# Third tile retrieved in the second merge, the table stage written out in turn, and another way of building the gate table

## The chip, the cores and the metric

The kernel runs on one core of one Trainium2 chip. The core has five engines that work side by side, each with its own queue of instructions: TensorE (PE in the profile; PEld is its loading of weights), VectorE (DVE), ScalarE (ACT), GpSimd (POOL) and SyncE (SP, which here only starts transfers). The metric is the device time of one execution in microseconds, as the median of several runs; less is better.

## The reference

The input is 1024 tokens of 1024 channels. A first half of the block (RWKV time mixing beside a sparse attention, merged by gates, then a LayerNorm) gives x; after it comes PEER, an expert layer with 16384 experts, of which each token takes 16 for each of 8 heads. The change bears on how this second part is scheduled and computed:

```python
merged = jax.nn.sigmoid(z_ga) * y_a + jax.nn.sigmoid(z_gb) * y_b
mix = merged @ w_out[l]
x = _layer_norm(DEEPNORM_ALPHA * x + gt1[:, None] * mix, ln1_g[l], ln1_b[l])
...
def _peer(h, w_pq, sub_keys, u_tab, v_tab):
    q = (ht @ w_pq).reshape(T, PEER_HEADS, 2, PEER_HALF)
    s = jnp.einsum('thcd,hcnd->thcn', q, sub_keys)           # 128 keys per half
    s1, i1 = lax.top_k(s[:, :, 0], 16)
    s2, i2 = lax.top_k(s[:, :, 1], 16)
    cand = s1[..., :, None] + s2[..., None, :]
    cand_idx = i1[..., :, None] * 128 + i2[..., None, :]
    top_s, pos = lax.top_k(cand, 16)                         # over 256 pairs
    experts = jnp.take_along_axis(cand_idx, pos, axis=-1)
    gates = softmax(top_s)
    act = gelu(einsum('cd,chkd->chk', hc, u_tab[experts])) * gates
    return einsum('chk,chkd->cd', act, v_tab[experts])
```

An expert's number is (first key i1) x 128 + (second key i2), and a gate is the weight that a token gives to one chosen expert.

## The kernel before

The tokens go in 8 tiles of 128. The first half of the block handles them in two halves of 512; each half ends in `merge(H)`, which multiplies the two branches by w_br_a and w_br_b, gates and adds them, multiplies by w_out, normalizes, and multiplies by the query weights wq (one column block per head h). PE multiplies in three terms (high and low part of weights and activations), here called three-term products.

Retrieval of a tile (`retrieve`, from L1117) is mostly DVE work in 6 steps: scores of the keys by PE, the best 16 of each half by MAX, MATCH_REPLACE and FIND_INDEX, sums of candidate pairs, their best 16, and then the keys i1 and i2 and the gates. The keys are found by `weighted`, which multiplies 0/1 marks by differences and sums each run of 16 by four halving additions (L1192, L1194 to L1196). The retrieval of a tile is a generator; `side` is a chain of such generators that other code advances a step at a time by `next(side)`. With M1 = 3, tiles up to 2 are retrieved inside the merges and tiles 3 to 7 afterwards.

The experts are then computed in two ways. For tiles 0 to 2 (384 tokens) expert rows are gathered: 768 indirect transfers, started by POOL (L1371), each of one row of 1024 numbers per token, each followed by one DVE instruction (L1375 for u, L1379 for v). Rows land in three rooms named g. Rows 0 to 127 run in the first half of the program, rows 128 to 299 in the table stage (below), the others in the dense stage. For tiles 3 to 7 (640 tokens) all experts are computed densely: for each of the 128 first keys i1, `dots_u` multiplies 128 experts' u by all 640 tokens (48 matmuls of 128x320, lines L1285, L1287, L1289), gelu and the gates of that i1 are applied, and `dense_v` multiplies by v (again 48 matmuls for each of 128 units). Weights come in as raw; ACT makes the high part whi and POOL the low part wlo.

The dense way needs a table of gates, indexed by i1, i2 and token. `gate_table` (from L1240) makes it in batches of 8 tokens: 80 batches for the 5 tiles. For each token it makes a row of 0 and 1 that marks i2 (one DVE instruction for all 8, L1247) and a row that holds the gate where the key is i1: six of the 8 tokens by one DVE instruction each (L1252), two by two ACT instructions each (L1254, L1255). A matmul per token (16 PE instructions per batch, L1259) multiplies the two into PSUM, ACT copies two times 128x512 to `st` (L233, st<-tp), and every fourth batch is written to memory (gtD).

The program after the first half has two stages. The table stage holds the retrieval of tiles 3 to 7, the gate table, rows 128 to 299, and the dots of 69 of the 128 first keys ("ahead"; results ds go to memory, dotD). The dense stage holds the other 59 dots, the 128 units of dense_v, and the other rows; it goes over 16 groups of 8 first keys. In each group it loads the gates by `gate_rows` (gt<-gtD).

The order on each engine is made by a scheduler in the build: it simulates times and takes, of what is ready, what stands first in the program. In the table stage the program has retrieval and table first, the 69 dots behind them, the rows last.

## Time and profile before

| what | value |
|---|---|
| runs, us | 3887.53, 4839.4, 3887.27; median 3887.53 |
| profiled execution, us | 3874.22, of which the trace spans 3872.5 |
| busy over the span: PE, DVE | 3549.4 (92%), 2759.5 (71%) |
| busy over the span: ACT, POOL | 1611.5 (42%), 1992.2 (51%) |
| granted clock, mean | 0.955 of full speed |

The trace is of one execution on this one core. A share of busy time is a mean over stages that differ, so the stages are read one by one. In the trace's own time the second merge fills the stretch 1483 to 1683 us, the table stage 1683 to 2469, and the dense stage 2469 to the end. A matmul of four-byte numbers outside the three-term products is two PE instructions in the trace.

### The profile page before, as it was taken

The numbers are of one execution on the slowest core, as the hardware profiler recorded it, in microseconds if no ns is written. First come the engines' busy times: TensorE is split into PE (matmuls) and PEld (weight loads), VectorE is DVE, ScalarE is ACT, GpSimd is POOL, SyncE is SP. The second block draws the span as 40 slices with busy tenths as digits, with TensorE's granted clock in tenths as the row PEclk, the third lists the DMA queues.
The fourth block names the chain that finished last, engine by engine and source line by source line (L and its number), as shares of the span: only waits on it lengthen the run. The fifth ranks groups of instructions, "written<-read, shape, count | busy, mean of one in ns | idle before, by whom it ended". The sixth has DMA issues, their size and how long they took to land.

```text
span 3872.5 us, 65040 instructions
## 1 busy us (share of the span) xinstructions
PE 3549.4 (92%) x24044; PEld 3172.0 (82%) x24045; DVE 2759.5 (71%) x5983; ACT 1611.5 (42%) x2909; POOL 1992.2 (51%) x1566
## 2 busy tenths in 40 slices
PE   8989999888999998779999898899999999999997
PEld 7667776665777776669889898899999999999997
DVE  7856644857377767779999999566676666676654
ACT  3558852343444443426455463622222232222222
POOL 5442222355455543254545454266676676776655
PEclk9999998999999999889999999999999999999998
DMA  7453334765676765477777777688898988998973
GB/s 231 148 151 103 103 98 143 280 188 183 192 222 219 218 220 170 140 258 261 243 259 252 258 273 248 234 301 314 310 332 317 330 313 323 335 323 318 322 266 115
DMA packets 434994, 920.97 MB, mean 238 GB/s; under 512 B 36356, under 2 KB 195412, under 8 KB 431732
## 3 DMA queue, kind: packets, MB, share of 16 engines
q1 hardware_dynamic: 311956, 498.38, 38.5%
q0 software_dynamic: 122720, 418.43, 31.0%
q8 instruction: 190, 3.11, 0.3%
q14 instruction: 128, 1.05, 0.1%
HBM read 791.59 MB, written 125.08 MB: 237 GB/s over the span
## 4 chain that ended last, share of the span: by engine, by line
PE 33%; DVE 21%; DMA 19%; issue 10%; POOL 9%; ACT 4%; SPq 1%; POOLq 0%; ACTq 0%; DVEq 0%
DMA g<-in_v_dram,gidx 4%; PE acc L425 4%; PE acc L426 4%; PE acc L427 4%; DMA g<-in_u_dram,gidx 4%; POOL g L1371 4%; POOL wlo L1272 4%; DVE pg L1379 3%; DMA raw<-in_vt_dram 3%; DMA gt<-gtD 3%; DVE gt L1252 3%; PE pair L1285 2%; PE pair L1287 2%; PE pair L1289 2%; DMA raw<-in_ut_dram 2%
## 5 line engine op out<-in xcount | busy, mean ns | idle before, releaser
L1272 POOL TENSOR_TENSOR wlo<-raw,whi 128x1024 fp32r<-128x1024 f32 x264 | 641.0, 2429 | 285.8 <-ACT whi L233 273.6
L415 POOL TENSOR_TENSOR wlo<-wraw,whi 128x512 fp32r<-128x512 f32 x280 | 372.5, 1333 | 564.0 <-ACT whi L233 496.7
L1371 POOL DMA_INDIRECT g<-in_u_dram,gidx x384 | 403.8, 1052 | 374.0 <-DVE g L1375 211.5
L1371 POOL DMA_INDIRECT g<-in_v_dram,gidx x384 | 388.0, 1011 | 378.3 <-DVE pg L1379 192.2
L1379 DVE SCALAR_TENSOR_TENSOR pg<-g,dots,pg 128x1024 f32<-128x1024 f32 x381 | 489.3, 1284 | 120.3 <-DMA g<-in_v_dram,gidx 113.9
L1285 PE MATMUL pair<-A,whi 128*128 128x320 f32 (+2 forms) x2048 | 483.0, 312 | 38.7 <-DVE A L1317 25.9
L1285 PE MATMUL pair<-h2T,whi 128*128 128x320 f32 x2048 | 479.1, 314 | 17.3 <-DMA h2T<-h2TD 10.0
L1287 PE MATMUL pair<-h2T,whi 128*128 128x320 f32 x2048 | 482.1, 315 | 3.7 <-DMA h2T<-h2TD 3.7
L233 ACT ACTIVATE whi<-raw 128x1024 fp32r<-128x1024 f32 x264 | 278.4, 1056 | 496.2 <-PE pair L1287 194.6
L1287 PE MATMUL pair<-A,whi 128*128 128x320 f32 (+2 forms) x2048 | 480.8, 311 | 0.0
L1289 PE MATMUL pair<-A,wlo 128*128 128x320 f32 (+2 forms) x2048 | 480.2, 311 | 0.5 <-POOL wlo L1272 0.5
L1289 PE MATMUL pair<-h2T,wlo 128*128 128x320 f32 x2048 | 480.4, 314 | 0.0
L1375 DVE SCALAR_TENSOR_TENSOR g<-g,pg 128x1024 f32<-128x1024 f32 x256 | 308.3, 1216 | 106.8 <-DMA g<-in_u_dram,gidx 104.6
L1285 PEld LDWEIGHTS pair<-A,whi 128*128 128x128 f32 x2048 | 348.8, 190 | 43.3 <-issue 29.6
L425 PE MATMUL acc<-big,whi 128*128 128x512 f32 x864 | 356.3, 413 | 23.5 <-DVE zs L533 7.1
L1285 PEld LDWEIGHTS pair<-h2T,whi 128*128 128x128 f32 x2048 | 348.3, 191 | 20.2 <-issue 11.0
L1287 PEld LDWEIGHTS pair<-h2T,whi 128*128 128x128 f32 x2048 | 349.5, 191 | 5.5 <-DMA h2T<-h2TD 4.0
L427 PE MATMUL acc<-big,wlo 128*128 128x512 f32 x864 | 350.7, 406 | 2.4 <-POOL wlo L415 2.4
L426 PE MATMUL acc<-big,whi 128*128 128x512 f32 x864 | 348.9, 404 | 3.6 <-DVE big L451 3.6
L1289 PEld LDWEIGHTS pair<-h2T,wlo 128*128 128x128 f32 x2048 | 348.8, 191 | 1.5
L1289 PEld LDWEIGHTS pair<-A,wlo 128*128 128x128 f32 x2048 | 348.8, 190 | 1.0 <-POOL wlo L1272 1.0
L1287 PEld LDWEIGHTS pair<-A,whi 128*128 128x128 f32 x2048 | 349.2, 190 | 0.0
(482 smaller groups left out, 6650.4 us busy)
## 6 DMA issues: line engine op xcount, KB each, us to landing
raw<-in_vt_dram SPq DMA_DIRECT2D x136, 512.0 KB
raw<-in_ut_dram SPq DMA_DIRECT2D x128, 512.0 KB
gtD<-st SPq DMA_DIRECT2D x20, 2048.0 KB
gt<-gtD SPq DMA_DIRECT2D x32, 1280.0 KB
wraw<-in_wz_dram SPq DMA_DIRECT2D x152, 256.0 KB
dotD<-ds SPq DMA_DIRECT2D x69, 320.0 KB
al<-dotD SPq DMA_DIRECT2D x69, 320.0 KB
mw<-in_wada_dram SPq DMA_DIRECT2D x32, 512.0 KB
```

Source lines behind the costliest of these rows:

```text
L233: copy = lambda o, i, **k: A.activation(o, i, AF.Copy, **k)
L415: G.tensor_tensor(lo, raw, hi.bitcast(F32), op=OP.subtract)
L425: mm(pt, lhsT=wh[:, ks], rhs=ah[:, k, :], start=k == 0, stop=False)
L426: mm(pt, lhsT=wh[:, ks], rhs=al[:, k, :], start=False, stop=False)
L427: ins = mm(pt, lhsT=wl[:, ks], rhs=ah[:, k, :], start=False, stop=k == nk - 1)
L1272: G.tensor_tensor(lo, raw, hi.bitcast(F32), op=OP.subtract)
L1285: mm(pts[n], lhsT=wh, rhs=ah[:, h], start=k == 0, stop=False)
L1287: mm(pts[n], lhsT=wh, rhs=al[:, h], start=False, stop=False)
L1289: mm(pts[n], lhsT=wl, rhs=ah[:, h], start=False, stop=last)
L1371: G.indirect_dma_start(out=u, out_offset=None, in_=a["u" if n < 2 else "v"], in_offset=bass.IndirectOffsetOnAxis(ap=idx[:, k:k + 1], axis=0))
L1375: V.scalar_tensor_tensor(u, u, 1.0, h2, op0=OP.mult, op1=OP.mult, accum_out=dots[:, k:k + 1])
L1379: V.scalar_tensor_tensor(acc, u, dots[:, k:k + 1], acc, op0=OP.mult, op1=OP.add)
```

## The change

- M1 goes from 3 to 4: tile 3 is retrieved in the second merge too. There the retrieval's steps stand after every second block of the merge (4 and 4), and one more after each of the 8 column blocks of wq, where before there were none.
- `weighted` sums each run of 16 by one TENSOR_REDUCE in place of four additions.
- `gate_table`: one DVE instruction per batch marks the first keys of all 8 tokens at once, in bf16, in a layout with the token innermost (hot; keys8 is a constant with each key 8 times). ACT then makes the 8 gate rows, one copy with a scale each, reading every eighth bf16 number. The matmuls write PSUM with a step of four numbers (`tp[:, :, t]`), and the copy to st reads PSUM in a row and writes runs of four numbers.
- The table stage is written out in turn: after each retrieval step three table batches, two dots and five gathered rows, and so on. Rows 128 to 299 get three more rooms, named gx. h2T, the activations that the dots multiply, is loaded by 8 transfers in place of 2.
- The dense stage no longer puts a first key that is not ahead at the head of each group.

```diff
-ONE_HOT = 6
-M1 = 3
+M1 = 4
+GX = 3
...
-            if H or d % QS == QS - 1:
+            if H == 0 or d % 2:
                 next(side, None)
...
-            next(side, None)
+            if H == 0 or d % 2:
+                next(side, None)
...
             nc.sync.dma_start(qTD[H][:, h, :], qt)
+            if H:
+                next(side, None)
...
-            V.tensor_tensor(pr[:, :, 0:8], pr[:, :, 0:8], pr[:, :, 8:16], op=OP.add)
-            s4 = tp_.tile([128, 64, 8], F32, name="wx")
-            V.tensor_tensor(s4[:, :, 0:4], pr[:, :, 0:4], pr[:, :, 4:8], op=OP.add)
-            V.tensor_tensor(s4[:, :, 0:2], s4[:, :, 0:2], s4[:, :, 2:4], op=OP.add)
-            V.tensor_tensor(dst, s4[:, :, 0], s4[:, :, 1], op=OP.add)
+            V.tensor_reduce(dst, pr, axis=AX.X, op=OP.add)
...
+    first_keys = lambda slots: slots[:, 2, 0:64].bitcast(BF)
...
-            oh = du.tile([128, 16, 128], F32, name="gt", bufs=2)
-            V.tensor_tensor(oh[:, 0:8], iota[:, None, :].to_broadcast([128, 8, 128]),
-                            slots[:, 1, b * 8:b * 8 + 8, None].to_broadcast([128, 8, 128]), op=OP.is_equal)
+            room = du.tile([128, 20, 128], F32, name="gt", bufs=2)
+            oh2, oh1 = room[:, 0:8], room[:, 8:16]
+            hot = room[:, 16:20].rearrange("p a b -> p (a b)").bitcast(BF).rearrange("p (a b) -> p a b", b=8)
+            V.tensor_tensor(hot, keys8, k1[:, None, b * 8:b * 8 + 8].to_broadcast([128, 128, 8]), op=OP.is_equal)
+            V.tensor_tensor(oh2, iota[:, None, :].to_broadcast([128, 8, 128]),
+                            slots[:, 0, b * 8:b * 8 + 8, None].to_broadcast([128, 8, 128]), op=OP.is_equal)
             for t in range(8):
-                c = slice(b * 8 + t, b * 8 + t + 1)
-                if t < ONE_HOT:
-                    V.tensor_scalar(oh[:, 8 + t], iotan, slots[:, 0, c], slots[:, 2, c], op0=OP.is_equal, op1=OP.mult)
-                else:
-                    A.activation(oh[:, 8 + t], iota, AF.Square, bias=slots[:, 0, c])
-                    A.activation(oh[:, 8 + t], oh[:, 8 + t], AF.Relu, scale=ng[:, c], bias=slots[:, 2, c])
+                copy(oh1[:, t], hot[:, :, t], scale=slots[:, 1, b * 8 + t:b * 8 + t + 1])
             for u in range(2):
-                tp = ptp()
+                tp = ptp().rearrange("p (a b) -> p a b", b=4)
                 for t in range(4):
-                    mm(tp[:, t * 128:(t + 1) * 128], lhsT=oh[:, 4 * u + t], rhs=oh[:, 8 + 4 * u + t], start=True, stop=True)
+                    mm(tp[:, :, t], lhsT=oh2[:, 4 * u + t], rhs=oh1[:, 4 * u + t], start=True, stop=True)
                 t0 = b % 4 * 8 + 4 * u
-                copy(s_[:, :, t0:t0 + 4].rearrange("p a b -> p b a"), tp.rearrange("p (b a) -> p b a", b=4))
+                copy(s_[:, :, t0:t0 + 4], tp)
...
+            if EARLY <= row < MIDDLE and row % (GB + GX) >= GB:
+                return at["sl"].tile([128, 1024], F32, name="gx", bufs=GX)
...
-        for n in range(2):
-            G.dma_start(h2T[:, n], h2TD[:, n])
+        for k in range(8):
+            G.dma_start(h2T[:, :, k], h2TD[:, :, k])
...
+            def beside(tables, dots, n):
+
                 for g in list(found.values()):
-                    for _ in range(3):
+                    for _ in range(tables):
                         next(g, None)
+                for _ in range(dots):
+                    next(ahead_, None)
+                for _ in range(n):
+                    next(rows)
...
+            for k in range(steps):
+                next(side)
+                beside(3, 2, n)
+            for _ in side:
+                pass
+            for k in range(8):
+                beside(2, 1, n if k < 6 else 0)
...
-                else:
-
-
-                    lead = next(i1 for i1 in first if i1 not in ahead)
-                    first = [lead] + [i1 for i1 in first if i1 != lead]
```

How the order moves shows at three places; these lists count a gate matmul once, so a batch is 8. The first is DVE in the middle of the table stage, before; gt is the room of the one-hot rows, v, s, i and cand belong to the retrieval, and pg is a gathered tile's sum.

```order
L1247 TENSOR_TENSOR gt<-iota,slots 128x1024
L1252 TENSOR_SCALAR gt<-iotan,slots 128x128
L1144 MAX_INDEX i_15924<-v_15923,s_16251 128x8
L1252 TENSOR_SCALAR gt<-iotan,slots 128x128
L1144 MAX_INDEX i_15924<-v_15923,s_16251 128x8
L1153 TENSOR_TENSOR cand<-v_15923 128x8x8
L1144 MAX_INDEX i_15924<-v_15923,s_16251 128x8
L1252 TENSOR_SCALAR gt<-iotan,slots 128x128 x2
L1144 MAX_INDEX i_15924<-v_15923,s_16251 128x8
L1150 TENSOR_TENSOR cand<-v_15923 128x8x16
L1252 TENSOR_SCALAR gt<-iotan,slots 128x128 x2
L1379 SCALAR_TENSOR_TENSOR pg<-g,dots,pg 128x1024
```

The same place on DVE with the change:

```order
L1393 SCALAR_TENSOR_TENSOR pg<-gx,dots,pg 128x1024
L1145 MAX_INDEX i_17628<-v_17627,s_17640 128x8 x3
L1249 TENSOR_TENSOR gt<-keys_15755,slots 128x1024
L1250 TENSOR_TENSOR gt<-iota,slots 128x1024
L1145 MAX_INDEX i_17628<-v_17627,s_17640 128x8
L1393 SCALAR_TENSOR_TENSOR pg<-gx,dots,pg 128x1024
L1393 SCALAR_TENSOR_TENSOR pg<-g,dots,pg 128x1024
L1249 TENSOR_TENSOR gt<-keys_15755,slots 128x1024
L1250 TENSOR_TENSOR gt<-iota,slots 128x1024
L1393 SCALAR_TENSOR_TENSOR pg<-g,dots,pg 128x1024
```

The six L1252 of a batch, strewn between the retrieval's instructions, are gone; a batch is one L1249 and one L1250, and gathered rows from both kinds of rooms stand between the batches.

The second place is PE between the last column of wq (acc) and the first dots (pair), before; L1127 are the retrieval's scores of the keys.

```order
L427 MATMUL acc<-Q,wlo 128x512
L1127 MATMUL tp<-keysT,qT 128x128 x12
L1285 MATMUL pair<-h2T,whi 128x320 x4
L1127 MATMUL tp<-keysT,qT 128x128 x4
L1287 MATMUL pair<-h2T,whi 128x320 x2
L1289 MATMUL pair<-h2T,wlo 128x320 x2
L1285 MATMUL pair<-h2T,whi 128x320 x2
```

The same place on PE with the change (L1233 are the transposes of a retrieved tile's keys and gates, which need its whole retrieval done):

```order
L425 MATMUL acc<-Q,wlo 128x512
L1233 MATMUL tp<-ident,i_15675 128x128
L1233 MATMUL tp<-ident,gates 128x128
L1233 MATMUL tp<-ident,i_15674 128x128
L1128 MATMUL tp<-keysT,qT 128x128 x4
L1284 MATMUL pair<-h2T,whi 128x320 x2
L1286 MATMUL pair<-h2T,whi 128x320 x2
L1288 MATMUL pair<-h2T,wlo 128x320 x2
```

The transposes of tile 3 now stand ahead of the first dots.

The third is PE at the end of the table stage, before; the rows behind the 128 gate matmuls are the first dots of the dense stage.

```order
L1285 MATMUL pair<-h2T,whi 128x320 x2
L1287 MATMUL pair<-h2T,whi 128x320 x2
L1289 MATMUL pair<-h2T,wlo 128x320 x2
L1259 MATMUL tp<-gt 128x128 x128
L1285 MATMUL pair<-h2T,whi 128x320 x2
L1287 MATMUL pair<-h2T,whi 128x320 x2
L1289 MATMUL pair<-h2T,wlo 128x320 x2
```

The end of the table stage on PE with the change:

```order
L1286 MATMUL pair<-h2T,whi 128x320 x2
L1288 MATMUL pair<-h2T,wlo 128x320 x2
L1284 MATMUL pair<-h2T,whi 128x320 x2
L1286 MATMUL pair<-h2T,whi 128x320 x2
L1288 MATMUL pair<-h2T,wlo 128x320 x2
L1258 MATMUL tp<-gt 128x128 x8
L1284 MATMUL pair<-h2T,whi 128x320 x2
L1286 MATMUL pair<-h2T,whi 128x320 x2
```

Before, the last 128 gate matmuls stand in one block behind all 69 dots of this stage; now they stand in pieces between the last dots.

## Rows read from the trace of the kernel before

**Rows 1.** Stages: length, busy time (instructions) by engine, clock, DMA share, GB/s.

```profile
1483.00:1683.00 200.00, 151.90 (x645) 116.61 (x643) 146.40 (x660) 79.06 (x136) 61.74 (x47) 0.85 0.49 160
1683.00:2469.00 786.00, 695.48 (x4731) 675.05 (x4731) 763.69 (x1920) 412.21 (x691) 367.44 (x239) 0.95 0.73 251
2469.00:3872.50 1403.50, 1337.90 (x9017) 1330.90 (x9016) 909.88 (x1130) 388.14 (x478) 921.66 (x672) 0.98 0.84 302
```

**Rows 2.** A wait of PE, table stage: waiter, what released it, us, times, longest.

```profile
PE tp L1236 <- DVE i L1196: 32.5, 8, 7.7
```

**Rows 3.** DVE groups, table stage: busy us, mean ns, idle before.

```profile
L1252 DVE TENSOR_SCALAR gt<-iotan,slots 128x128 f32<-128x128 f32 x480 | 190.6, 472 | 0.0
...
L1379 DVE SCALAR_TENSOR_TENSOR pg<-g,dots,pg 128x1024 f32<-128x1024 f32 x127 | 162.7, 1281 | 6.8 <-DMA g<-in_v_dram,gidx 6.1 <-DVE wp L1190 0.2
...
L1247 DVE TENSOR_TENSOR gt<-iota,slots 128x1024 f32<-128x1024 f32 x80 | 104.9, 1311 | 2.8 <-ACT gt L1255 2.8
...
L1194 DVE TENSOR_TENSOR wx<-wp 128x256 f32<-128x256 bf16 x30 | 30.1, 1002 | 0.7
L1192 DVE TENSOR_TENSOR wp<-wp 128x512 bf16<-128x512 bf16 x30 | 25.2, 839 | 0.4
L1195 DVE TENSOR_TENSOR wx<-wx 128x128 f32<-128x128 f32 x30 | 23.7, 790 | 0.7
...
L1184 DVE TENSOR_TENSOR ge<-wx,ranks 128x1024 bf16<-128x1024 bf16 x20 | 13.8, 692 | 0.5
...
L1196 DVE TENSOR_TENSOR i<-wx 128x64 f32<-128x64 f32 x20 | 13.7, 683 | 0.2
...
L1214 DVE TENSOR_REDUCE gs<-gates 128x8 f32<-128x128 f32 x5 | 1.4, 285 | 0.7 <-ACT gates L1212 0.7
```

**Rows 4.** PE and ACT groups, table stage.

```profile
L1259 PE MATMUL tp<-gt 128*128 128x128 f32 x1280 | 177.2, 292 | 52.8 <-DVE gt L1252 40.0 <-ACT st L233 12.8
...
L233 ACT ACTIVATE st<-tp 128x512 f32<-128x512 f32 x159 | 164.7, 1110 | 118.9 <-PE tp L1259 118.4
...
L233 ACT ACTIVATE whi<-raw 128x1024 fp32r<-128x1024 f32 x70 | 73.8, 1054 | 98.9 <-PE pair L1287 65.9 <-issue 25.0 <-DMA raw<-in_ut_dram 5.7
L1255 ACT ACTIVATE gt<-gt,slots,ng 128x128 f32<-128x128 f32 x160 | 70.4, 489 | 8.0 <-DVE ng L1243 7.7 <-ACT ds L233 0.3
...
L1254 ACT ACTIVATE gt<-iota,slots 128x128 f32<-128x128 f32 x160 | 52.6, 386 | 0.0
...
L233 ACT ACTIVATE ds<-pair 128x640 f32<-128x640 f32 x69 | 47.4, 687 | 0.0
...
L233 ACT ACTIVATE slots<-tp 128x128 f32<-128x128 f32 x5 | 1.4, 273 | 17.9 <-PE tp L1236 17.9
```

**Rows 5.** PE timeline, gate batch among dots: start us, us, instructions.

```profile
1995.85 1.95 PE L1259 MATMUL tp<-gt 128*128 128x128 f32 x16
1997.55 0.39 PE L1285 MATMUL pair<-h2T,whi 128*128 128x320 f32 x1
1997.78 0.46 PE L1287 MATMUL pair<-h2T,whi 128*128 128x320 f32 x2
...
1999.83 0.46 PE L1289 MATMUL pair<-h2T,wlo 128*128 128x320 f32 x2
```

**Rows 6.** PE timeline, the last gate batches of the table stage.

```profile
2418.58 3.78 PE L1259 MATMUL tp<-gt 128*128 128x128 f32 x16 [4.67 <-DVE gt L1252]
...
2467.01 2.05 PE L1259 MATMUL tp<-gt 128*128 128x128 f32 x16 [0.97 <-ACT st L233]
```

**Rows 7.** A stretch inside the second merge, columns as in group 1.

```profile
1490.00:1580.00 90.00, 74.01 (x309) 55.84 (x308) 89.11 (x465) 31.34 (x55) 27.73 (x20) 0.91 0.43 134
```

**Rows 8.** PE timeline at the start of the table stage.

```profile
1679.81 1.40 PE L1285 MATMUL pair<-h2T,whi 128*128 128x320 f32 x4 [10.02 <-DMA h2T<-h2TD]
```

**Rows 9.** Waits of PE, dense stage.

```profile
PE pair L1285 <- DVE A L1317: 29.5, 16, 6.6
```

**Rows 10.** Waits of DVE, dense stage.

```profile
DVE pair L1315 <- DMA gt<-gtD: 85.1, 16, 18.2
```

More of the change, by code (lines that the diff above doesn't have):

```diff
@@ L1369, in peer_gather @@
                     idx = index(row)
-                u = grow() if row < MIDDLE or row % (GB + GM) < GB else dv.tile([128, 1024], F32, name="g2", bufs=GM)
+                u = room(row)
                 G.indirect_dma_start(out=u, out_offset=None, in_=a["u" if n < 2 else "v"],
@@ L1407, in out_rows, with finish @@
         nc.sync.dma_start(out[r0:r0 + n, :], dst[p])
-    def finish(i, acc, dv, rows):
+    def finish(i, acc, at):
         last = i == NG - 1
-        row, xa = ((dv.tile([128, 2 * DN], F32, name="A", bufs=AB)[:, 0:1024] if last else grow()) for _ in range(2))
+        row, xa = ((at["dv"].tile([128, 2 * DN], F32, name="A", bufs=AB)[:, 0:1024] if last else grow()) for _ in range(2))
         mod_row(row, 2)
@@ L1417, in finish @@
         V.tensor_tensor(y2, y2, xa, op=OP.add)
-        g, b = rows[0:2] if last else (grow(), grow())
+        g, b = at["ln"][0:2] if last else (grow(), grow())
         if not last:
@@ L1608, in body @@
             st = sl.tile([128, 2, 128, 32], F32, name="st")
+            keys8 = sl.tile([128, 128, 8], BF, name="keys8")
+            copy(keys8, iota[:, :, None].to_broadcast([128, 128, 8]))
             found = {}
@@ L1618, in body, with dots_ahead @@
             side = retrieve_all(range(M1, 8), tk, table)
-            live = True
-            while live:
-                live = next(side, side) is not side
+            more = {"du": du, "sl": sl, "pg": pg}
+            rows = gather_all(more)
+            for _ in range(EARLY):
+                next(rows)
+            def dots_ahead():
+                for i1 in ahead:
+                    ds = sl.tile([128, DN], F32, name="ds", bufs=4)
+                    copy(by_half(ds), dots_u(i1, du, h2T, 2))
+                    nc.sync.dma_start(dotD[ahead[i1]], ds)
+                    yield
+            ahead_ = dots_ahead()
+            def beside(tables, dots, n):
                 for g in list(found.values()):
-                    for _ in range(3):
+                    for _ in range(tables):
                         next(g, None)
+                for _ in range(dots):
+                    next(ahead_, None)
+                for _ in range(n):
+                    next(rows)
+            steps = 6 * (8 - M1)
+            n = (MIDDLE - EARLY) // (steps + 6)
+            for k in range(steps):
[5 more added lines that the diff above has]
+                beside(2, 1, n if k < 6 else 0)
+            for _ in range(MIDDLE - EARLY - n * (steps + 6)):
+                next(rows)
             for g in found.values():
@@ L1627, in body @@
                     pass
-            mark("dots")
-            for i1 in ahead:
-                ds = sl.tile([128, DN], F32, name="ds", bufs=4)
-                copy(by_half(ds), dots_u(i1, du, h2T, 2))
-                nc.sync.dma_start(dotD[ahead[i1]], ds)
+            for _ in ahead_:
+                pass
         tkp.__exit__(None, None, None)
@@ L1671, in body @@
             mark("gather")
-            for i in range(NG):
-                finish(i, peer_gather(i, du, dv, pg), dv, ln)
+            more.update(dv=dv, ln=ln)
+            for _ in rows:
+                pass
     mark("end")
```

37 lines of the change are left out of this document (22 added, 15 removed).

## The prediction

> **What bounds the kernel now.** I read the table by stages first [rows 1]: what is to be seen there is which engine has no time left. In the dense stage it is PE: 1337.9 of 1403.5 us busy, at 0.98 of full clock. In the table stage it is DVE: 763.7 of 786 us (97%), while PE is busy for 695.5 and ACT for 412.2. So the table stage is the place where less DVE work can show in the time, and in the dense stage it can't.
>
> The second view is what PE waits for in the table stage [rows 2, 4]: 40.0 us for one-hot rows by L1252, and 32.5 us for the last addition of the retrieval's sums (L1196); both are DVE. The third is what the same PE work needs when nothing holds it. In the timeline [rows 5] seven pairs of dots' matmuls start between 1997.78 and 1999.83: 2.05 / 14 = 0.146 us each, so 48 x 0.146 = 7.03 us for a unit of dots, and a gate batch between them takes 1997.55 - 1995.85 = 1.70 us. The stage has 69 dots and 80 batches: 485 + 136 = 621 us. That is 79% of its 786. The dense stage has 59 + 128 = 187 units, 1315 us, which is 94% of its 1403.5 [rows 1]. The gap between 79% and 94% is what there is to win. The last place to look at is the end of the table stage [rows 6]: from 2418.58 to 2469 PE has gate batches alone, 16 of them for 27 us of work, at first held by DVE and then by ACT's copies to st (a batch each 3.05 us: 2.05 of work and 0.97 of waiting).
>
> **The change part by part: DVE in the table stage.** Taken out: 190.6 us of L1252; 25.2 + 30.1 + 23.7 + 13.7 = 92.7 us of halving additions [rows 3]; and tile 3's share of the rest of the retrieval, which is what 763.7 leaves without these, the one-hot rows of L1247 (104.9) and the gathered rows of L1379 (162.7): 212 us for five tiles. Added: 80 marks of first keys (128x1024 in bf16) and 24 reduces for four tiles. A mark is nearest to L1184, the comparison of 128x1024 bf16, 0.69 us; its f32 cousin L1247 takes 1.31, so 55 to 105 us, and I take 55. No reduce of 128x1024 is shown; the small one, L1214 with 128x128, takes 0.285 us, and eight of these would be 2.28; the cheapest pass over 1024 numbers is 0.69. So 17 to 55 us, and I take 31 (1.3 each, as L1247, which also goes through f32). With a fifth of 212 us gone, DVE comes to 764 - 191 - 93 + 55 + 31 - 42 = about 525 us (at the upper prices 600). That is below PE's 621 in either case, so DVE stops being the bound, and PE or ACT comes next.
>
> **ACT in the table stage.** Taken out: 52.6 + 70.4 us of L1254 and L1255 and 164.7 us of copies to st, which leaves 124.5. Added: 640 copies of one gate row, and 160 copies to st in the new order [rows 4]. A copy with a scale of 128x128 that reads PSUM in a row takes 0.273 us (slots<-tp); the two activations on 128x128 take 0.386 and 0.489. The copy to st now takes 1.11 us for 512 numbers written with a step of 128 bytes, while ds takes 0.687 us for 640 numbers in a row, so 0.55 for 512: the step costs (1.11 - 0.55) / 512 = 1.1 ns a number. I take the same for the new read, which steps by 16 bytes: 0.273 + 0.14 = 0.41 us, in a range from 0.27 to 0.53, and 0.55 for the new copy to st in a range from 0.55 to 1.11. A batch then takes ACT 8 x 0.41 + 2 x 0.55 = 4.4 us (3.3 to 6.5), all 80 of them 350 us, and ACT comes to 475 of some 690. [...]
>
> What counts is the stretches with gates. In the changed order of PE 20 of the 69 dots have no gate matmul near them, so the 80 batches lie beside 49 dots. PE needs 49 x 7.03 + 136 = 480 us there; ACT 80 x 4.4 + 49 x (1.05 + 0.69) for whi and ds = 437. PE is late by a little, so the new ACT work is hidden, but narrowly; at 6.5 us a batch it would be 605 and not hidden.
>
> **PE in the table stage.** Its work stays as it is, if a matmul that writes PSUM with a step of four costs what it did. No matmul of before does that, so the bounds are 0 and a doubling. The block of 16 batches at the end gets dots between its pieces, which takes its 28 us of waiting. With DVE at 525 and ACT at 475, I take a share of 90% for PE's 621: between now and the dense stage, nearer to the latter, as score matmuls, transposes and some waits for the retrieval stay. 621 / 0.90 = 690 us, **96 us less**. By the dense stage's 94% it is 661, by 86% it is 722.
>
> **The gathered rows** are as many as before. POOL has 367.4 of 786 us of work and DVE now has room; the six rooms let loads run ahead, which is worth nothing as neither is the bound. The same bytes in 690 us are a DMA share of 0.73 x 786 / 690 = 0.83, which the dense stage has already (0.84) [rows 1]. Zero, then, between -5 and +10.
>
> **Second merge and the start of the dots.** From 1490 to 1580 DVE is busy for 89.1 of 90 us and PE for 74.0 [rows 7], so retrieval steps hold the merge there. Half of them move behind wq's columns; PE can gain its 16 us, and up to some 25 with the stretches around. Then the first dots wait for h2T, 10.0 us in one piece at 1679.81 [rows 8], loaded as two large pieces; eight pieces by k let the first products start at the first one. Against it: tile 3's transposes stand ahead of the first dots, so PE waits for its whole retrieval, a third one in a stretch that had two. A tile's retrieval is (212 + 93) / 5 = 61 us of DVE before, and the stretch of wq in which DVE had little to do is shorter than that. So I give the first dots 13 us and not 25, in a range from -28 to +7.
>
> **Dense stage.** Without the reordering, each group begins with ahead keys. PE loses 29.5 us in 16 waits for A [rows 9], most of them behind DVE's wait for the gates' load (85.1 us in 16, [rows 10]), because before a group's first key and the ahead ones came from two different loads. That load now has the time of a few units more. But the unit of dots at the group's head, 7 us, which covered gelu and gates of the others, is gone. I take -10, in a range from -30 to +15.
>
> **Sum.** -96 - 13 - 10 = -119, and two microseconds back for rounding of stages that overlap: -117. The profiled execution of 3874.2 becomes 3757, and the median of the runs, which is 13.3 us above it, 3887.5 - 117 = **3770** us. With the ends of the terms together, taken as partly independent, this forecast goes from 3715 to 3825.
>
> **Rivals.** First, the written step makes the gate matmuls dearer (slower than before). For it: the operation is new, and 1280 instructions stand on the bounding engine. Against it: in the timeline a gate instruction of 128 columns takes 0.106 us beside dots that take 0.146 for 320 columns [rows 5], so these matmuls aren't limited by the pace of their columns' writes alone. With k times the price the stage is (485 + 136k) / 0.90: at k = 2 that is 841, +55, less 23 for the other two parts: about +32, **3920**. From k = 1.8 on it eats the whole gain. [...]
>
> Second, ACT becomes the bound where the gates are. At the upper price the 49 dots with gates take 605 in place of 480 us: the stage is 690 + 125 = 815, and with the other parts the time is 3887.5 + 29 - 23 = 3894; at 5.4 us a batch (8 x 0.53 + 2 x 0.55) it is 517, +37, which is 3807. I give this case, at its middle, **3850**. For it: the price of a read by steps isn't shown, and ACT works in order, so whi for the next dots queues behind eight gate rows. Against it: the 40.0 us of waiting for DVE falls away whatever ACT does.
>
> Third, the change does less than it says: tile 3 holds PE at the start for the 30 us that DVE needs, and the first dots come at 1700 in place of 1670: **3800**.
>
> **How the numbers follow.** A measurement of this kernel can tell about 2% from no change, which is 78 us: faster is below 3810, slower above 3965. The forecast has 0.66, the second rival 0.13, the third 0.09, the first 0.12. Faster: nine tenths of the forecast, a third of the second rival and most of the third: 0.71. Slower by over 2% needs k above 2.3 in the first rival: 0.04. Same is the rest, 0.25. The range is 3715 to 3850: it takes in the forecast's own range, the third rival and the milder half of the second.
>
> **What would show it.** Right: the table stage is 690 us long, DVE is busy for near 525 of it, PE's share is 0.90, no wait for one-hot rows by DVE is left, and no block of gate batches stands alone at the end. A gate row by ACT takes 0.41 us and a copy to st 0.55. Wrong: a gate batch that takes 3 us and more on PE without any wait (first rival); PE's waits on gt released by ACT, above 50 us in sum (second); a PE wait of 20 us and more for tile 3's keys, ahead of the first dots (third). A dense stage that grows by over 15 us would show that the head of each group was worth more than the gate load's wait.

## The result, and the profile after

The changed kernel takes 3747.99 us in the median of four runs (3743.65 to 3754.99), the kernel before 3889.49. The ratio is 0.964, 95% interval 0.9619 to 0.966: faster by 3.6%, 141.5 us where 117 were forecast. The ratio leaves out the one execution of the kernel before that took 4839.4 us. The profiled execution went from 3874.22 to 3743.65 us, its span from 3872.5 to 3741.9, which is 130.6 us; two later comparisons, each beside the kernel before, gave 128 and 127 us (a_changed and e6 in the table below).

The table of stages of the kernel after has the columns of [rows 1]: length, busy time and instructions of PE, PEld, DVE, ACT and POOL, granted clock, DMA share, GB/s. The upper bounds are the same event, the end of what stands ahead of the dense stage. The lower ones are not quite: 1677 is the start of the first dots, while 1683 of before lies 3.2 us behind it (1679.81, [rows 8]), and 1483 is a round number in both.

```profile
1483.00:1677.00 194.00, 144.13 (x625) 109.30 (x623) 172.54 (x751) 84.54 (x143) 69.19 (x55) 0.85 0.57 185
1677.00:2367.00 690.00, 664.00 (x4734) 650.02 (x4735) 569.68 (x1294) 490.03 (x1002) 349.14 (x235) 0.99 0.78 281
2367.00:3741.90 1374.90, 1333.36 (x9008) 1329.82 (x9006) 915.10 (x1130) 387.68 (x477) 924.51 (x673) 0.99 0.86 307
```

Beside [rows 1] the table stage is shorter by 96 us (786 to 690; from the first dots on it is 789 to 690), the dense stage by 28.6 (1403.5 to 1374.9). The 6 us of the second merge (200 to 194) are not what the merge gained, as is shown below. DVE is busy for 569.7 of 690 us, 83% and no longer 97%. PE's idle time in the table stage went from 786 - 695.5 = 90.5 to 690 - 664 = 26 us; the other 31.5 us are less busy time for nearly as many instructions (4731 and 4734), at a granted clock of 0.99 in place of 0.95. The clock can be most of that, by an estimate from these rows: 695.5 x 0.95 / 0.99 = 667. But a gate batch that stands alone also counts as busy for longer (2.05 us) than one between dots (1.70) [rows 5, 6], so the share of the clock isn't shown. In the dense stage 24 of the 28.6 us are idle time of PE.

The costliest groups of the table stage after, as in [rows 3, 4] (busy us, mean ns, idle before):

```profile
L232 ACT ACTIVATE gt<-gt,slots 128x128 f32<-128x128 bf16 x640 | 274.4, 517 | 62.3 <-DVE gt L1249 55.9 <-issue 2.5 <-DVE i L1145 1.9
...
L1258 PE MATMUL tp<-gt 128*128 128x128 f32 x1280 | 161.7, 279 | 14.2 <-ACT st L232 11.5 <-ACT sc L232 2.5
...
L232 ACT ACTIVATE st<-tp 128x512 f32<-128x512 f32 x160 | 87.4, 586 | 24.0 <-PE tp L1258 22.0 <-issue 1.5 <-PE pair L1286 0.4
L1393 DVE SCALAR_TENSOR_TENSOR pg<-gx,dots,pg 128x1024 f32<-128x1024 f32 x64 | 81.9, 1280 | 3.0 <-DMA gx<-in_v_dram,gidx 2.4
...
L1249 DVE TENSOR_TENSOR gt<-keys,slots 128x1024 bf16<-128x1024 bf16 x80 | 67.8, 852 | 50.5 <-issue 21.9 <-ACT gt L232 18.8 <-PE tp L1258 7.5
...
L1193 DVE TENSOR_REDUCE i<-wp 128x64 f32<-128x1024 bf16 x16 | 19.4, 1214 | 0.3
```

A gate row by ACT takes 0.517 us from its start to its end, but the rows of a batch overlap: 274.4 us for 640 are 0.43 each. A copy to st takes 0.586 us in place of 1.110 (87.4 / 160 = 0.55 with the overlap), a mark 0.85, a reduce 1.21. PE's 40.0 us of waiting for one-hot rows is gone; 14.2 us are left, nearly all for ACT. DVE hardly waits for rows of experts (3.0 us in the row of gx). It now waits for ACT, 31.4 us for the retrieval's scores (sc) and 18.8 for gate rows in L1249's row:

```profile
DVE v L1137 <- ACT sc L232: 31.4, 12, 5.6
```

At the start of the stage PE's timeline and its waits, from 1460 to 1677, show the third rival's wait:

```profile
1643.52 0.40 PE L425 MATMUL acc<-Q,wlo 128*128 128x512 f32 x1
...
1674.93 0.45 PE L1233 MATMUL tp<-ident,i 128*128 128x128 f32 x1 [31.01 <-DVE i L1193]
```

```profile
PE tp L1233 <- DVE i L1193: 31.0, 1, 31.0
```

wq's products end at 1643.9 (1664.9 before), and then PE stands for 31.0 us until tile 3's keys are there. The wait for h2T [rows 8] is hidden behind it. Of the 21 us between these two ends 6.3 lie ahead of the merge, whose first product starts at 1483.9 before and at 1477.6 here. They can't be put down to the change: in a_changed, the changed kernel run again, it starts at 1485.8. Counted from its first product, the merge up to the end of wq, and then the time to the first dots, are, before:

```profile
1483.90:1664.90 181.00, 146.12 (x607) 112.11 (x605) 132.04 (x563) 73.83 (x125) 53.04 (x40) 0.87 0.44 141
1664.90:1679.80 14.90, 2.32 (x24) 1.80 (x25) 13.80 (x94) 4.68 (x9) 7.76 (x6) 0.68 0.92 341
```

and after:

```profile
1477.60:1643.90 166.30, 147.44 (x637) 111.88 (x635) 147.60 (x702) 75.92 (x133) 52.52 (x40) 0.92 0.50 157
1643.90:1676.90 33.00, 1.99 (x13) 1.44 (x12) 27.79 (x55) 10.52 (x13) 19.26 (x17) 0.55 0.94 331
```

The merge gains 14.7 us and the wait takes 18.1, so the first dots come 3.4 us later in the merge's own time (6 in a_changed).

In the dense stage PE's wait for A (the dense activations, made of dots and gates), 29.5 us in 16 before [rows 9], is now

```profile
PE pair L1284 <- DVE A L1316: 18.3, 8, 4.3
```

and DVE's waits there have no row for gt's load any more [rows 10]. PE's wait for A is 11 of the 24 us of idle time; what the rest was stays open.

### The profile page after: what moved, and what is told of

Read it like the earlier page. It is cut to its first block, busy times and chain, and to the rows that moved or that the text cites. A ratio compares the mean times of both kernels' runs of the same rounds, so it can differ in the third digit from the quotient of the medians.

```text
span 3741.9 us, 64784 instructions
## 1 busy us (share of the span) xinstructions
PE 3505.2 (94%) x24045; PEld 3139.0 (84%) x24045; DVE 2596.4 (69%) x5433; ACT 1695.7 (45%) x3230; POOL 1981.3 (53%) x1572
## 3 DMA queue, kind: packets, MB, share of 16 engines
q0 software_dynamic: 124608, 418.43, 31.4%
## 4 chain that ended last, share of the span: by engine, by line
PE 49%; DVE 14%; DMA 13%; issue 8%; POOL 7%; ACT 6%; SPq 0%; POOLq 0%; ACTq 0%; DVEq 0%
PE pair L1284 7%; PE pair L1286 7%; PE pair L1288 7%; PE acc L423 4%; PE acc L424 4%; PE acc L425 4%; POOL g L1385 3%; DMA g<-in_u_dram,gidx 3%; DMA raw<-in_vt_dram 3%; POOL wlo L1271 3%; DMA g<-in_v_dram,gidx 3%; PE tp L1258 2%; DMA raw<-in_ut_dram 2%; ACT gt L232 2%; PE acc L975 2%
## 5 line engine op out<-in xcount | busy, mean ns | idle before, releaser
L1385 POOL DMA_INDIRECT g<-in_u_dram,gidx x361 | 373.6, 1035 | 298.4 <-DVE g L1389 180.5
L1393 DVE SCALAR_TENSOR_TENSOR pg<-g,dots,pg 128x1024 f32<-128x1024 f32 x317 | 407.1, 1284 | 123.1 <-DMA g<-in_v_dram,gidx 118.0
L1284 PE MATMUL pair<-h2T,whi 128*128 128x320 f32 x2048 | 475.6, 312 | 0.2 <-ACT ds L232 0.2
L1286 PE MATMUL pair<-h2T,whi 128*128 128x320 f32 x2048 | 473.3, 311 | 0.0
L1385 POOL DMA_INDIRECT g<-in_v_dram,gidx x320 | 307.7, 961 | 170.8 <-DVE pg L1393 80.8
L1389 DVE SCALAR_TENSOR_TENSOR g<-g,pg 128x1024 f32<-128x1024 f32 x233 | 281.0, 1216 | 118.4 <-DMA g<-in_u_dram,gidx 116.8
L1284 PEld LDWEIGHTS pair<-h2T,whi 128*128 128x128 f32 x2048 | 344.6, 189 | 1.6 <-ACT ds L232 0.4
L1286 PEld LDWEIGHTS pair<-h2T,whi 128*128 128x128 f32 x2048 | 343.9, 189 | 1.0
```

Source lines behind the costliest of these rows:

```text
L1284: mm(pts[n], lhsT=wh, rhs=ah[:, h], start=k == 0, stop=False)
L1286: mm(pts[n], lhsT=wh, rhs=al[:, h], start=False, stop=False)
L1385: G.indirect_dma_start(out=u, out_offset=None, in_=a["u" if n < 2 else "v"], in_offset=bass.IndirectOffsetOnAxis(ap=idx[:, k:k + 1], axis=0))
L1389: V.scalar_tensor_tensor(u, u, 1.0, h2, op0=OP.mult, op1=OP.mult, accum_out=dots[:, k:k + 1])
L1393: V.scalar_tensor_tensor(acc, u, dots[:, k:k + 1], acc, op0=OP.mult, op1=OP.add)
```

## Experiments

For each kernel the table gives medians and ratios, and of its profiled execution "first dots" (start of the first product on h2T) and "first A" (start of the first copy of a dense activation); between them lies the table stage. The first row is the kernel before, in the trace of [rows 1]; a_changed is the changed kernel once more. The first dots of one and the same kernel differ by 11 us from execution to execution (changed and a_changed), mostly by what lies ahead of the second merge, so the lengths of stages say more than the starts.

| kernel | median us | ratio to before, 95% | first dots | first A | table stage | first A to end |
|---|---|---|---|---|---|---|
| before | | | 1679.8 | 2484.9 | 805.1 | 1387.6 |
| changed | 3747.99 | 0.9640, 0.9619 to 0.9660 | 1676.9 | 2377.9 | 701.0 | 1364.0 |
| a_changed | 3749.20 | 0.9663, 0.9626 to 0.9699 | 1688.1 | 2389.9 | 701.8 | 1356.8 |
| e1_late_transposes | 3736.41 | 0.9643, 0.9615 to 0.9671 | 1649.1 | 2353.7 | 704.6 | 1357.4 |
| e10_late_again | 3738.77 | 0.9642, 0.9603 to 0.9682 | 1659.5 | 2366.6 | 707.1 | 1359.1 |
| e2_old_gate_table | 3788.53 | 0.9774, 0.9745 to 0.9802 | 1689.4 | 2421.7 | 732.3 | 1373.2 |
| e3_lead_back | 3774.62 | 0.9737, 0.9707 to 0.9766 | 1687.3 | 2384.1 | 696.8 | 1392.6 |
| e4_tile3_back | 3776.12 | 0.9728, 0.9692 to 0.9763 | 1659.0 | 2404.1 | 745.1 | 1367.3 |
| e5_new_gates_alone | 3891.62 | 1.0051, 1.0028 to 1.0073 | 1681.2 | 2499.4 | 818.2 | 1390.2 |
| e12_retrieval_alone | 3815.28 | 0.9837, 0.9816 to 0.9858 | 1678.8 | 2417.6 | 738.8 | 1383.9 |
| e9_old_turn | 3776.72 | 0.9735, 0.9694 to 0.9775 | 1679.7 | 2414.2 | 734.5 | 1358.3 |
| e8_three_rooms | 3783.12 | 0.9746, 0.9726 to 0.9766 | 1686.1 | 2423.4 | 737.3 | 1364.7 |
| e7_old_sums | 3789.32 | 0.9772, 0.9750 to 0.9794 | 1701.6 | 2419.3 | 717.7 | 1364.4 |
| e6_contiguous | 3750.28 | 0.9662, 0.9632 to 0.9693 | 1684.6 | 2385.8 | 701.2 | 1365.6 |

Three groups ran side by side with the kernel before: e1, e2, e3, e5 (before 3875.17 us), a_changed, e4, e9, e10 (3877.39), and e6, e7, e8, e12 (3877.50). e6 is the changed kernel but for a layout that cost nothing (0.9662 beside a_changed's 0.9663), and stands for it in its group.

**The gate table: e2 and e5.** e2 is the changed kernel with the old table:

```diff
-            V.tensor_tensor(hot, keys8, k1[:, None, b * 8:b * 8 + 8].to_broadcast([128, 128, 8]), op=OP.is_equal)
...
-                copy(oh1[:, t], hot[:, :, t], scale=slots[:, 1, b * 8 + t:b * 8 + t + 1])
+                if t < ONE_HOT:
+                    V.tensor_scalar(oh[:, 8 + t], iotan, slots[:, 0, c], slots[:, 2, c], op0=OP.is_equal, op1=OP.mult)
+                else:
+                    A.activation(oh[:, 8 + t], iota, AF.Square, bias=slots[:, 0, c])
+                    A.activation(oh[:, 8 + t], oh[:, 8 + t], AF.Relu, scale=ng[:, c], bias=slots[:, 2, c])
...
-                    mm(tp[:, :, t], lhsT=oh2[:, 4 * u + t], rhs=oh1[:, 4 * u + t], start=True, stop=True)
+                    mm(tp[:, t * 128:(t + 1) * 128], lhsT=oh[:, 4 * u + t], rhs=oh[:, 8 + 4 * u + t], start=True, stop=True)
```

> The changed kernel, all but the gate table, which is the one of before (six of eight gate rows by DVE, two by ACT in two instructions, PSUM written in a row). Theory (the table stage was bound by DVE's work): DVE's 570 us in the stage lose 68 and get 191, so 693, which is the whole of the present 690; the stage grows to about 725 to 735 and the time to 3780 to 3795. Rival (the order written out in turn gave the gain): the stage stays within 10 us of 690 and the time within 10 of the changed kernel's 3748.

3788.53 us, as the first theory had it: the stage is longer by 31 us (701 to 732), a little less than the 35 to 45 expected. The windows of e2's table stage, and PE's waits there:

```profile
1689.40:2421.70 732.30, 687.54 (x4802) 672.82 (x4801) 693.52 (x1699) 410.30 (x684) 361.45 (x236) 0.97 0.77 267
```

```profile
PE tp L1258 <- DVE gt L1251: 31.7, 15, 3.5
```

DVE is busy for 693.5 of 732.3 us (693 expected) and PE waits for its gate rows again. Against a_changed's ratio the old table costs 0.0111 x 3876 = 43 us in this order. e5 is the other half, the kernel before with nothing but the new table:

```diff
-                if t < ONE_HOT:
-                    V.tensor_scalar(oh[:, 8 + t], iotan, slots[:, 0, c], slots[:, 2, c], op0=OP.is_equal, op1=OP.mult)
...
+            V.tensor_tensor(hot, keys8, k1[:, None, b * 8:b * 8 + 8].to_broadcast([128, 128, 8]), op=OP.is_equal)
...
+                copy(oh1[:, t], hot[:, :, t], scale=slots[:, 1, b * 8 + t:b * 8 + t + 1])
```

> The kernel before with the new gate table alone (marks of first keys in one DVE instruction, gate rows by ACT, PSUM written by steps); order, M1, sums, rooms and dense stage as before. Theory: DVE's work in the table stage falls from 764 to about 640, and the dots with gates beside them run at PE's pace; but 16 batches still stand alone at the end, and there ACT needs 8 x 0.517 + 2 x 0.586 = 5.3 us a batch, 85 us in place of 55. The stage comes to 715 to 740, the time to 3820 to 3845. Rival (the order gave the gain): stage above 765, time above 3868. If the block at the end doesn't matter: stage near 690 and time near 3790.

It is slower than before (1.0051). Here my theory fell: DVE has 631.7 us of work in place of 765, and the stage is 818 us in place of 805. What PE and DVE wait for, in e5's table stage:

```profile
PE tp L1261 <- ACT st L233: 38.9, 22, 5.3
PE tp L1236 <- DVE i L1196: 35.1, 5, 11.4
```

```profile
DVE pg L1381 <- DMA g<-in_v_dram,gidx: 49.9, 26, 5.4
...
DVE g L1377 <- DMA g<-in_u_dram,gidx: 17.0, 9, 5.8
```

PE waits for ACT where it waited for DVE, and as long (38.9 us for 40.0). DVE, with time of its own, now stands for 66.9 us on rows of experts that haven't landed, where before it was 11.2 us:

```profile
DVE pg L1379 <- DMA g<-in_v_dram,gidx: 6.1, 5, 2.0
DVE g L1375 <- DMA g<-in_u_dram,gidx: 5.1, 4, 2.2
```

And the block at the end is worse than it was in [rows 6]; PE's timeline:

```profile
2467.17 2.05 PE L1261 MATMUL tp<-gt 128*128 128x128 f32 x16 [0.47 <-ACT st L233]
2471.49 2.05 PE L1261 MATMUL tp<-gt 128*128 128x128 f32 x16 [2.26 <-ACT st L233]
2475.76 2.80 PE L1261 MATMUL tp<-gt 128*128 128x128 f32 x16 [2.22 <-ACT st L233]
2480.02 3.78 PE L1261 MATMUL tp<-gt 128*128 128x128 f32 x16 [1.46 <-ACT st L233]
```

A batch there takes 4.27 us, which is ACT's eight gate rows and two copies (5.3 were expected, from the times of single ones, which overlap), where one of before took 3.05: for the 16 batches that is some 20 us. Less work on the busiest engine gave nothing. I read this as three other things standing close behind it: ACT's rows in the block, rows that land late, and the end of the retrieval. e5 alone doesn't show it; the runs below undo them one by one.

**The retrieval: e12, e4, e7.** e12 is the kernel before with the retrieval's edits alone:

```diff
-M1 = 3
+M1 = 4
...
+            if H:
+                next(side, None)
...
-            V.tensor_tensor(pr[:, :, 0:8], pr[:, :, 0:8], pr[:, :, 8:16], op=OP.add)
...
+            V.tensor_reduce(dst, pr, axis=AX.X, op=OP.add)
```

> The kernel before with the retrieval's edits alone: M1 = 4, the merge's steps in their new places, sums by one reduce; the gate table, the order of the table stage, three rooms, h2T's two loads and the dense stage as before. The block of 16 gate batches behind the last dots is gone from its order of PE. Theory B (the stage of before was as long as the retrieval took, plus that block; either gets shorter only by less retrieval work in the stage): from first dots to first A 735 to 765 us in place of 805, less what PE waits for tile 3 at the start (25 to 35 us, in place of 14 for h2T), ratio 0.980 to 0.992. Theory D (DVE's work is what counts, and the gate rows were most of it): DVE still has 191 us of gate rows, some 660 in all, and the stage stays above 780, ratio above 0.993.

0.9837 and a stage of 738.8 us: theory B, with the old gate rows still on DVE. The block is gone (the last gate batch starts at 2346.7, with dots behind it up to the stage's end), and of the 127 us of e6, beside it, these edits alone give 62. PE's waits in e12's table stage and ahead of it:

```profile
PE tp L1235 <- DVE i L1195: 36.3, 9, 22.7
PE tp L1258 <- DVE gt L1251: 31.0, 23, 3.1
```

PE still waits for DVE's gate rows (31.0 us), as in e2. e4 puts only tile 3 back into the table stage of the changed kernel:

```diff
-M1 = 4
+M1 = 3
```

> The changed kernel with M1 = 3: tile 3 is retrieved in the table stage again, all else as changed, the stage written out in turn too. In its order of PE the last 128 gate matmuls stand in one block again. Theory B (tile 3's earlier retrieval is what shortened the stage): the block costs what it costs in the kernel before with the new gate table, 16 x 4.3 = 68 us for 27 of work; DVE has one more retrieval to do; the table stage comes to 745 to 790, ratio 0.975 to 0.988. Theory A (the order written out in turn did it): stage within 15 us of 701, ratio within 0.004 of the changed kernel's.

The stage is 745 us (theory B), and the block is there again, in PE's timeline:

```profile
2377.97 2.89 PE L1258 MATMUL tp<-gt 128*128 128x128 f32 x16 [2.23 <-ACT st L232]
2382.23 3.74 PE L1258 MATMUL tp<-gt 128*128 128x128 f32 x16 [1.37 <-ACT st L232]
2386.49 2.05 PE L1258 MATMUL tp<-gt 128*128 128x128 f32 x16 [0.52 <-ACT st L232]
```

But the first dots come 29 us earlier, since no transposes stand ahead of them. So the ratio rose by 0.0065, 27 us, less than theory B's low end: tile 3's earlier retrieval gives 43 us in the stage and pays 29 for it at the start. That leaves 14 us at the first A; from there to the end e4 takes another 10.5 more than a_changed, for which no cause is shown. e4 also has the merge's new places and h2T's eight transfers without tile 3: its first dots come 177.1 us after the merge's first product, 195.9 before and 199.3 in the changed kernel. What each of these two edits gives wasn't tested by itself. e7 is the changed kernel with the old sums:

```diff
-            V.tensor_reduce(dst, pr, axis=AX.X, op=OP.add)
+            V.tensor_tensor(pr[:, :, 0:8], pr[:, :, 0:8], pr[:, :, 8:16], op=OP.add)
...
+            V.tensor_tensor(dst, s4[:, :, 0], s4[:, :, 1], op=OP.add)
...
```

> The changed kernel with the four halving additions in place of one reduce. DVE gets about 3 us more for each of 24 sums in the table stage (four additions of 3.1 us in all for one reduce of 1.2, some 45 us in the stage) and some 6 sums' worth, 11 us, on the path of tile 3 ahead of the first dots. Theory: with DVE at 570 of 701 us only the start shows: 8 to 14 us, ratio higher by 0.002 to 0.004. Rival (the retrieval's own length still sets the stage): 25 us and more, ratio higher by 0.007.

39 us more than e6, beside it: the time is the rival's. The sums lengthen the retrieval itself, and PE waits for its end at each tile:

```profile
PE tp L1237 <- DVE i L1197: 63.4, 5, 42.8
```

63.4 us in 5, the first 42.8, against 42.3 in 5 with 33.6 in e6. The first dots are 17 us later than in e6, of which 5 lie ahead of the merge, and the stage is 16.5 longer, though DVE is busy for only 581 of its 718 us.

**Rooms and turn: e8 and e9.** e9 has the table stage in the old writing, and three rooms; e8 has the new writing and three rooms:

```diff
-GX = 3
+GX = 0
...
```

and e9 besides, with the rows written behind the dense stage:

```diff
...
+            live = True
+            while live:
+                live = next(side, side) is not side
                 for g in list(found.values()):
-                    for _ in range(tables):
+                    for _ in range(3):
                         next(g, None)
...
-            for k in range(steps):
-                next(side)
-                beside(3, 2, n)
...
+            for i1 in ahead:
+                ds = sl.tile([128, DN], F32, name="ds", bufs=4)
+                copy(by_half(ds), dots_u(i1, du, h2T, 2))
+                nc.sync.dma_start(dotD[ahead[i1]], ds)
...
+            for _ in gather_all({"du": du, "pg": pg, "dv": dv, "ln": ln}):
```

> The changed kernel, with the table stage written as before (retrieval and tables first, then the 69 dots, all gathered rows at the end of the program, three rooms in place of six); M1 = 4, sums, gate table, h2T's loads and the dense stage are the changed ones. In its order of PE no block of gate batches stands at the end. Theory A (writing the stage out in turn is what shortened it): the table stage, 701 us from first dots to first A, grows to 750 or more, ratio above 0.977. Theory B (tile 3's earlier retrieval did it, since the retrievals then end while dots are left to put between the last batches): stage below 725, ratio below 0.971.

> The changed kernel with three rooms for rows in the table stage in place of six, the order written out in turn. The kernel with the old order and three rooms was 27 us behind the changed one. Theory A (the turn is what counts): the same time as the changed kernel, within 5 us. Rival (the rooms are what counts, since a DVE instruction on a row that hasn't landed holds up the retrieval and the marks behind it): 15 to 25 us more, and DVE's waits for rows above 40 us in the table stage.

e9's stage of 734.5 us lies between its two theories. e8 settles it: 737.3 us, as slow as e9, so with three rooms writing the stage out in turn gives nothing, and the rooms are worth 36 us of stage (33 us of time against e6). DVE's waits in the middle of e8's stage:

```profile
DVE pg L1393 <- DMA g<-in_v_dram,gidx: 54.5, 30, 7.5
...
DVE g L1389 <- DMA g<-in_u_dram,gidx: 20.2, 10, 5.7
```

74.7 us in 40 waits on rows that haven't landed, in which DVE stands idle with the retrieval and the marks queued behind the row. With six rooms the changed kernel has 3.9 us of it; from 1700 to 2370, the window of e8's rows, a_changed has 2.8 and e6 1.6. With three rooms e5 has 66.9 us in its stage, and e12 23.6 from 1700 to 2370 with DVE busy for 672 of its stage's 739 us; the kernel before, with DVE busy for 765 of 805 us, has 11.2. Whether six rooms would do the same with the rows written last wasn't tried.

**The dense stage: e3.**

```diff
+                else:
+                    lead = next(i1 for i1 in first if i1 not in ahead)
+                    first = [lead] + [i1 for i1 in first if i1 != lead]
```

> The changed kernel with the dense stage's old order inside a group: the first key that is not ahead stands first again. The dense stage got 28.6 us shorter with the change (1403.5 to 1374.9). Theory: the order inside the groups did it (29.5 us of PE waits for A in 16 became 18.3 in 8, and clock dips behind these waits went): dense stage 1390 to 1403, time 3765 to 3775. Rival: a steadier table stage and fewer transfers at the stage's start did it: dense stage stays within 8 us of 1375, time within 8 of 3748.

From first A to the end it takes 1392.6 us, 28.6 more than the changed kernel, and the wait for gates is back:

```profile
DVE pair L1314 <- DMA gt<-gtD: 62.9, 15, 7.1
```

```profile
PE pair L1284 <- DVE A L1316: 37.9, 13, 4.3
```

That is as the theory had it, and by the ratios the old order costs (0.9737 - 0.9663) x 3876 = 29 us. The table above agrees without exception: the four kernels with the old order in a group need 1383.9 to 1392.6 us there, the others 1356.8 to 1373.2.

**PSUM written by steps: e6.**

```diff
-                tp = ptp().rearrange("p (a b) -> p a b", b=4)
+                tp = ptp().rearrange("p (b a) -> p b a", b=4)
...
-                    mm(tp[:, :, t], lhsT=oh2[:, 4 * u + t], rhs=oh1[:, 4 * u + t], start=True, stop=True)
+                    mm(tp[:, t, :], lhsT=oh2[:, 4 * u + t], rhs=oh1[:, 4 * u + t], start=True, stop=True)
...
-                copy(s_[:, :, t0:t0 + 4], tp)
+                copy(s_[:, :, t0:t0 + 4], tp.rearrange("p b a -> p a b"))
```

> The changed kernel with the gate matmuls writing PSUM in a row and ACT's copy to st reading it by steps of 128 numbers, st's layout unchanged. In the changed kernel's trace a gate batch written by steps of four numbers takes 1.70 us of PE beside dots, as it did written in a row. Theory (the step of the write costs PE nothing): a batch takes 1.70 us again; the copy to st gets 0 to 0.5 us dearer than 0.586, which ACT has room for: ratio within 0.003 of the changed kernel's. Rival (the step costs PE, hidden by how matmuls overlap): a batch below 1.6 us and the time 8 us or more lower.

The same time as a_changed (0.9662 and 0.9663). A gate batch and the matmul behind it in PE's timeline, by steps (changed kernel) and in a row (e6), 1.70 us each:

```profile
2000.99 1.95 PE L1258 MATMUL tp<-gt 128*128 128x128 f32 x16
2002.69 0.39 PE L1284 MATMUL pair<-h2T,whi 128*128 128x320 f32 x1
```

```profile
2007.73 1.95 PE L1258 MATMUL tp<-gt 128*128 128x128 f32 x16
2009.43 0.39 PE L1284 MATMUL pair<-h2T,whi 128*128 128x320 f32 x1
```

Gate matmuls and copies to st in e6:

```profile
L1258 PE MATMUL tp<-gt 128*128 128x128 f32 x1271 | 162.1, 280 | 14.1 <-ACT st L232 11.3 <-ACT sc L232 2.7
...
L232 ACT ACTIVATE st<-tp 128x512 f32<-128x512 f32 x160 | 87.4, 586 | 21.6 <-PE tp L1258 21.5
```

280 ns for a matmul that writes in a row, 279 by steps; 586 ns for a copy that reads PSUM by steps, 586 in a row.

**The wait at the start: e1, e10 and a_changed.**

```diff
+LATE = 3
...
-                side = retrieve_all(range(1, M1), tk, by_slots)
+                late = {}
+                side = retrieve_all(range(1, M1), tk, late.__setitem__)
...
             ahead_ = dots_ahead()
+            for _ in range(LATE):
+                next(ahead_)
+            for i in late:
+                if i >= NG:
+                    table(i, late[i])
```

> The changed kernel with the transposes of tile 3 put behind the first three dots in the program, so that PE no longer waits for tile 3's retrieval before its first product of the table stage. In the trace of the changed kernel PE idles 31.0 us there, while h2T's eight loads are issued from 1651 on and the first dots start at 1677. Theory: the wait is real time on the path; dots start near 1657 and run at the pace of h2T's loads until about 1670, so the time falls by 10 to 18 us, to about 3733. Rival: the wait only moves (h2T, or the gates of tile 3, come no earlier and PE waits later for the same retrieval): within 4 us of the changed kernel.

> The changed kernel as it is, so that the kernels beside it have it on the same chip. Both theories: 0.964 of the kernel before, within 0.004.

> The kernel with tile 3's transposes behind the first dots once more, now on the same chip as the changed kernel. In its first trace the wait for tile 3 was gone (31.0 us), one of 15.0 us for h2T stood in its place, and the first dots began 15 us after the end of wq's products in place of 33. Theory: 10 to 18 us faster than the changed kernel (ratio to before lower by 0.003 to 0.005). Rival (the time comes back later in the stage): ratio within 0.0015 of the changed kernel's.

e1 alone could tell nothing, since the changed kernel hadn't run beside it (0.9643 and 0.9640). Side by side, e10 is 10.4 us faster than a_changed in the median, at the near end of what was expected; the ratio is lower by 0.0021, between the two theories, and the intervals overlap. The traces lean to the theory: the first dots come 28.6 us earlier and the first A 23.3, of which 8.4 are an earlier last product of wq in this execution (1644.2 for 1652.6), and these lie ahead of the merge (first product at 1477.4 for 1485.8). In place of the wait for tile 3 PE's waits now show

```profile
PE pair L1285 <- DMA h2T<-h2TD: 16.3, 3, 14.9
```

so half of the 31 us only changes its owner, and about 15 us at the first A are left to the edit in these two executions. By its medians this is the fastest version here; that it beats the changed kernel is likely and not shown.

## Why the prediction was right, and where it wasn't

The time lies in the range and 22 us below the forecast; two of its terms miss in opposite directions, which is luck. By its steps:

- **The table stage, -96 us**, came out as -96 between the bounds that the prediction used (-99 from the first dots), and PE's share, 621 of 690, as 90%. That is luck in part: the 90% was chosen between two known shares and not worked out from the waits or the clock. The end of the lone block at the stage's end is right. ACT has 490 us (475 forecast), with 0.43 us for a gate row in its batch (0.41) and 0.55 for a copy to st (0.55). DVE has 570 (525 forecast, 600 at the upper prices): a mark takes 0.85 us in place of 0.69, which is 13 of the 45 us, and the 212 us called retrieval held 44 gathered u rows too (L1375, 52.9 us), so that tile 3's fifth was some 11 us less. A reduce takes 1.21 (1.3).
- **The reason given for it was half of one.** The sentence "so DVE stops being the bound, and PE or ACT comes next" puts the gain on DVE's sum of busy time. e5 takes most of that work away and gains nothing. The stage is set by several chains through DVE's one queue: the length of the retrieval (e12, e7), its end against the last dots (e4), the gate rows (e2), and rows that land late (e8). Each of them binds once the others are mended, so what they give one by one doesn't add up: undone singly, gates, M1, sums and rooms cost 43, 27, 39 and 33 us, 142 us in all, where the whole change gave 128 (a_changed) and 127 us (e6), some 29 of them in the dense stage (e3).
- **The six rooms, costed at zero** ("worth nothing as neither is the bound"), are the step that failed: 33 us. The cover that I named, a DVE with room, is what exposed the loads: with three rooms the DVE of before, busy for 765 of 805 us, found its rows landed but for 11.2 us of waits, and a DVE with less work waited for them (66.9 us in e5, 74.7 in e8).
- **Merge and start, -13**, had the wrong sign: +3.4 from the merge's first product to the first dots (195.9 to 199.3; 202.3 in a_changed). The merge gained 14.7 us, a little less than the 16 to 25 forecast, and tile 3's keys kept PE for 31.0 us, so the time from wq to the first dots grew by 18.1. That is the third rival's wait, which eats the whole gain of the merge. The 6.3 us by which the merge began earlier in this trace are no part of it.
- **Dense stage, -10**, was mis-sized: -28.6 (-23.6 from first A to the end). The head of a group, which I thought to lose 7 us of cover, wasn't missed; e3 gives back 29 us.
- **The first rival** (stepped writes to PSUM) doesn't happen: a batch takes 1.70 us beside dots, as in [rows 5] and e6, and a gate matmul of 128 four-byte columns 279 ns where e6, which writes in a row, has 280. **The second rival** (ACT bounds the stretches with gates) is there in e5 and e4, where batches stand alone, at 4.27 and 4.26 us each, and is hidden in the changed kernel, in which PE waits for st 11.5 us.

It stays open how much of the table stage's gain each edit "has": they overlap, and the answer depends on which is taken first.

## What to carry to other kernels

When one engine's queue serves several chains, its busy share does not say what relieving it is worth (in e5 DVE's work fell from 765 to 631.7 us and the stage grew from 805 to 818): take one chain's work away by itself and look at what the engine then waits for. Relieving an engine can turn hidden loads into waits (11.2 us before, 66.9 in e5, 3.9 in the changed kernel with its six rooms), so give the loads more rooms in the same step. A block of small work that one engine can only feed slowly belongs between large work of the other engine (a gate batch took 4.27 us alone in e5, 1.70 between dots in the changed kernel), which means that its inputs must be ready before the large work runs out.

## What the runs showed of the hardware

- These matmuls of 128 columns took 279 ns with a write to PSUM by steps of four numbers (changed) and 280 in a row (e6); ACT's copy of 512 numbers to st took 586 ns with a read of PSUM by steps of 128 numbers (e6) and 586 in a row (changed). The same copy with its writes to SBUF by steps of 128 bytes took 1110 ns [rows 4], where with runs of four it took 586.
- ACT's gate row, a read of 128 bf16 numbers 16 bytes apart with a scale from a column, took 0.517 us from start to end, or 0.43 of ACT's time, as the rows of a batch overlap. A copy of 128 numbers from PSUM in a row, without such a scale, took 0.273, the activation L1254 with one operand from a column 0.386 [rows 4]. What the step alone costs isn't shown.
- From first dots to first A the granted clock was 0.93 with 102 us of PE's idle time (e5), 0.94 with 92 (before), 0.97 with 50 (e4), 0.98 with 44 (e9) and 0.99 with 26 (changed): lower where the gaps were longer, though not strictly (0.97 with 45 in e2, 0.98 with 47 in e8). That the gaps are its cause wasn't tested by itself.
